# Start addresses of the tiles that TensorE reads, in one hybrid decoder layer on one core

## The chip, the core and the metric

The kernel runs on one core of one Trainium2 chip. The metric is the device time of one execution in microseconds (us). The kernel before took 2267.95 us, the median of three runs (2267.1 to 2267.99).

## What is computed

One decoder layer over 512 tokens of width 2048, in float32. Cut to what matters here:

```python
h = rmsnorm(x, attn_norm)                       # x: [512, 2048]
proj = h @ w_in                                 # 2048 x 5376: q, k, v of head groups A, B, C
# A: windowed softmax attention, B: stick-breaking attention, C: dilated softmax attention
mix = concat(rmsnorm(out_a), rmsnorm(out_b), rmsnorm(out_c))
x = x + mix @ w_out                             # 2048 x 2048
u = causal_dwconv(rmsnorm(x, ffn_norm) @ w_up)  # 2048 x 11264
gate, up = split(u)
x = x + (silu(gate) * up) @ w_down              # 5632 x 2048
```

The four weight products carry nearly all of the matrix work.

## The kernel before

**Products in three parts.** TensorE takes float32r operands (float32 whose low bits are cleared). Each weight and each activation is therefore split into a high part and the rest, and each product of two 128-row tiles is three matmuls: high by high, high by rest, rest by high (function mm3, lines 263 to 267). The stationary operand of a matmul is a 128x128 block of weights (512 bytes in each partition, out of a tile wh or wl of 2048 bytes), the moving operand is a 128x512 tile of activations (2048 bytes in each partition), and the result is one PSUM tile, 512 columns wide.

**The order of the work.** One stream of weight products runs from start to end: the projections of B, A and C, the output projection, and the feed-forward layer in six chunks of eight tiles, up-products and down-products taken in turns. The pieces of the weights (512 KB) are loaded by SyncE's queue (SP) into three buffers wr; ScalarE (ACT) copies half a piece into wh, VectorE (DVE) subtracts it from the raw weights into wl (function split, lines 251 to 261). Attention, norms and the gating run beside this stream. A planner at build time (classes Engine and Clock, lines 38 to 114) gives every instruction an estimated duration and issues each side task when its inputs should be ready, so the order on every engine is fixed when the program is built. The planner's cost of an instruction depends on its kind and its columns, not on an address.

**Which tiles move through TensorE.** The trace names tiles without numbers. In the projections of the heads (up to about 650 us) and in the output projection for the heads of A and B, the moving tiles are `x`: 32 tiles of 2048 bytes in pool xp. In the output projection for the heads of C they are `mc` (16 tiles in pool fp). In the feed-forward layer the up-products move `xg2`, which the trace prints as `xg` (32 tiles in pool fp); the down-products move `x` for the chunks 0, 2 and 4 and `mc` for 1, 3 and 5 (line 992). In attention the tiles st and akv (queries and keys), pt (weights of attention), vt and av (values), sq (squares), and the constant matrices trir, restr, bdr and cst are read.

**Where the tiles lie.** The framework lays the tiles of a pool one behind another in the order in which they are first made, each rounded up to 32 bytes, and pool behind pool in the order cp, wp, xp, then ap (attention), whose place fp takes over after attention. The first 1152 bytes of a partition are the framework's own. In cp stand sm (240 bytes, rounded to 256), cst (1536), trir, restr, bdr (512 each), r1 (2048), epsc, onec, gp (one slot of 32 bytes each) and two gacc (2048 each), so wp begins at 10720. Worked out in this way, the tiles start at these offsets:

| tiles | pool | first start | past a multiple of 512 | past a multiple of 2048 |
|---|---|---|---|---|
| wh, wl (stationary, blocks at steps of 512) | wp | 23008 | 480 | 480 |
| x (moving) | xp | 39392 | 480 | 480 |
| xg2 (moving) | fp | 106336 | 352 | 1888 |
| mc (moving) | fp | 178016 | 352 | 1888 |
| st, sq (moving; st also stationary) | ap | 106976 | 480 | 480 |
| pt, akv, vt, av (after the small tile tb of 96 bytes) | ap | 154176 | 64 | several |
| trir, restr, bdr, cst (stationary) | cp | 1408 | 384 | several |

xg2 and mc differ from x because fp begins with the tile conv, whose 1408 bytes are no multiple of 512.

Of the kernel before, what the change touches and what calls it, by code (L numbers as in the profile page):

```python
# [9 lines left out]
F32 = mybir.dt.float32  # L10
F32R = mybir.dt.float32r
# [9 lines left out]
EPS = 1e-6  # L21
NEG = -1e30

# columns of the packed small parameters
SM_AG, SM_FG, SM_MG, SM_G4, SM_SINK, SM_CONV, SM_N = 0, 16, 32, 48, 52, 60, 60 + 88 * 4
# columns of the packed constants
C_ID, C_ONE, C_MASK, C_TRI = 0, 128, 256, 384
NB = 640
# the least spacing of the heads of A, B, C, and what is added to each estimate
GAP = (8, 10, 10)  # L30
MARGIN = 0.08
# the order of the units of A and C
ORDER = "ACACACACCCCC"
# the order in which the output projection takes the tiles of heads: B, A, C
MIX_ORDER = list(range(4, 8)) + list(range(4)) + list(range(8, 16))


class Engine:
    """An engine whose instructions are timed by estimate as they are issued."""

# [38 lines left out]
class Clock:  # L79
    """Issues tasks beside the stream of matrix products, in the order of the estimated times:  # L80
    a task yields when what it has issued has to end before it goes on (or a time to wait)."""

# [34 lines left out]
def program(tc, xT, w_in, w_out, w_up, w_down, small, table, consts, onehot, lognum, out):  # L117
# [24 lines left out]
    with ExitStack() as ctx:  # L142
# [14 lines left out]
        trir = cp.tile([128, 128], F32R, name="trir")  # L157
        restr = cp.tile([128, 128], F32R, name="restr")
        bdr = cp.tile([128, 128], F32R, name="bdr")
        r1 = cp.tile([128, S], F32, name="r1")  # L160
        epsc = cp.tile([128, 1], F32, name="epsc")
        onec = cp.tile([128, 1], F32, name="onec")
        gp = cp.tile([128, 4], F32, name="gp")
        gacc = [cp.tile([128, S], F32, name="gacc", bufs=2) for _ in range(2)]
        gacc.append(gacc[1])

        # a slot is taken before its tile is made and given back after the tile's last use
        total = {"pj": 2, "s": 4, "po": 1, "c": 1, "qs": 3, "st": 9, "akv": 4, "vt": 2, "av": 1, "strip": 2,
                 "sc": 3, "pt": 6, "sq": 6, "o": 2, "mx": 3, "dn": 3, "nm": 3, "es": 2,
                 "cv": 3, "acc": 1, "rg": 1}  # L170
        # the shapes of the slots that are not rows
        shapes = {"sc": [128, 1280], "pt": [128, 1664], "vt": [128, 4, 2, 2, 64], "av": [128, 4, 2, 2, 64],
# [31 lines left out]

# [1 line left out]
        b_units = [(10 + p, 6 + p, 14 + p) for p in range(4)]  # L206
# [25 lines left out]
        raws, parts = {}, {}  # L232
# [9 lines left out]
        def split_next():  # L242
            """the next half of a piece of the weights"""
            i = at["split"]
            if i // 2 < len(stream):
                at["split"] = i + 1
                raw, arrival = raws[i // 2]
                n = raw.shape[1] // 2
                spawn(split(raw[:, i % 2 * n:i % 2 * n + n], arrival, i))
# [24 lines left out]
        def accumulate(pt, acts, ks, each=None):  # L274
            """the k tiles ks of a tile of a product, with the next weights of the stream"""
            half = min(len(acts), 8) // 2
            for k in ks:
                while acts[k] not in ready:
                    idle()
                if k % half == 0:  # L280
                    while at["use"] not in parts:
                        idle()
                    hi, lo = parts.pop(at["use"])
                    at["use"] += 1
                    split_next()
                mm3(pt, hi, lo, k % half, ready[acts[k]], k == 0, k == len(acts) - 1)
                if each:
                    each(k)
                clock.run()

        def product(acts, after):
            """one tile of a product; then the task after(tile)"""
            pt = begin()
            accumulate(pt, acts, range(len(acts)))
            spawn(after(pt))
            clock.run()

# [1 line left out]
        def rstd(pool, ss, n):  # L299
            """-2n * (ss / n + EPS) ** -0.5, with a Newton step after the tables"""  # L300
            y, a = yield from take(pool, "sq", 2)
            scalar.activation(y, ss, AF.Ln, bias=epsc, scale=1.0 / n)
            scalar.activation(y, y, AF.Exp, scale=-0.5)
            yield
            gpsimd.tensor_mul(a, y, y)
            yield
            vector.scalar_tensor_tensor(a, ss, n * EPS, a, op0=ALU.add, op1=ALU.mult)
            give(ss)
            vector.scalar_tensor_tensor(a, a, -3.0 * n, y, op0=ALU.add, op1=ALU.mult)
            give(y)  # L310
            return a
# [26 lines left out]

        nc.scalar.preload_act_table_set("natural_log_exp_and_others")
        vector.memset(epsc, EPS)  # L340
        vector.memset(onec, 1.0)

# [1 line left out]
        with ExitStack() as actx:  # L344
            ap = actx.enter_context(tc.tile_pool(name="ap", bufs=1))

            def strips():
                """the biases of the heads that softmax takes, in their order, as far ahead as there is room"""
                for head in strip_order:
                    g = yield from take(ap, "strip")  # L350
                    a = rb[head:head + 1, 0:1]
                    load(g, bass.AP(tensor=a.tensor, offset=a.offset, ap=[[1, 128], [1, S]]))
                    yield
                    ready["strip", head] = g
# [8 lines left out]
            def stacked(q, key):  # L363
                """for each head of the pair its high parts over its low parts"""
                res = yield from take(ap, "st", 2, F32R)
                for h in range(2):
                    scalar.copy(res[h][HALF[h]], q[HALF[h]])
                yield
                for h in range(2):
                    vector.tensor_sub(res[h][HALF[1 - h]], q[HALF[h]], res[h][HALF[h]].bitcast(F32))  # L370
                give(q)
                yield
                ready[key] = res

            def doubled(q, key):
                """for each head of the pair its high parts twice and its low parts twice"""
                tag = "akv" if key[0] == "ak" else "st"
# [87 lines left out]
            def softmax_head(q, dup, vt, h, o, head, sinks, window):  # L465
# [53 lines left out]
                def place(t, i, n):  # L519
                    if window:  # L520
                        # block (j, i) at 256 j + 128 (i - j), the last one after its zeros
                        base, step = ((0, 128), (128, 128), (384, 128), (640, 256))[i]
                    else:
                        # block (j, i) at 384 j + 128 i
                        base, step = 128 * i, 384
# [33 lines left out]

            # key blocks j of the stick-breaking heads: (j, first query, number of queries, column); in the operands of  # L560
            # products the last block follows columns of zeros
            BLK = [(0, 0, 512, 0), (1, 128, 384, 512), (2, 256, 256, 896), (3, 384, 128, 1152)]
# [82 lines left out]

            # heads in the order in which they run, at most three at a time
            heads = []
# [44 lines left out]
            def spill(g):  # L692
                """the normalised heads of a group in high and low parts, to wait for the slots of x"""
                tiles = (range(4), range(4, 8))[g]
# [30 lines left out]

            # x and the first three tiles of w_in, tile of x by tile of x
            acc = grab(ap, "o")
# [116 lines left out]
            def last_products(q_after, v_after):  # L844
                """the last two tiles, by halves of x, so that half of its slots are free early"""
                q, v = begin(), begin()
# [29 lines left out]

            # the output projection of the heads of B and A, beside the last heads of C
            xn = []
# [22 lines left out]
            while left[2]:  # L901
# [3 lines left out]
                else:  # L905
                    idle()
# [1 line left out]
        fp = ctx.enter_context(tc.tile_pool(name="fp", bufs=1, reuse_waits="tile"))  # L908
        cv = fp.tile([128, SM_N - SM_CONV], F32, name="conv")
        load(cv, small[:, SM_CONV:])  # L910

# [46 lines left out]

# [1 line left out]
        gs = {}  # L960
# [84 lines left out]
def _pieces(w):  # L1045
    """[K, N] as pieces of eight K tiles by one N tile, each [128, 8 * 128]"""
    k, n = w.shape
# [50 lines left out]
```

## Time and profile before

| | |
|---|---|
| median of three runs | 2267.95 us |
| profiled execution: its span, first to last instruction | 2265.6 us |
| what lies around the span, against the median | 2.35 us |
| TensorE busy, share of the span | 2254.7 us, 100% |
| matmuls | 10068 |
| VectorE busy; ScalarE busy | 1211.2 us, 53%; 981.9 us, 43% |
| granted TensorE clock, mean | 1.000 |

The span is that of one profiled execution; beside it only the run times are given. A matmul's own duration in the trace (about 395 ns for 512 columns) overlaps its neighbours', because matmuls are pipelined, so "TensorE busy" says only that one is always under way. What TensorE takes for a matmul is the step from the start of one to the start of the next, read from the starts in the timeline or from a piece of the chain divided by its count. The granted clock of 1.0 is 2.4 GHz; if one column is taken in each cycle, as the planner reckons (line 62: 4 ns and n/2400 us), 512 columns are 213.3 ns, and the step cannot be shorter than that.

### The profile page before, as it was taken

The page shows a single profiled execution, that of the slowest core. Times are in us where ns is not written, and L with a number is a line of the kernel's source. Part 1 is how long each engine was busy: PE and PEld are TensorE (multiplying, and loading weights), DVE is VectorE, ACT ScalarE, POOL GpSimd, SP SyncE. Part 2 cuts the span into 40 slices and gives each one's busy share as a digit, 9 for nine tenths or more (in the row PEclk, how much of TensorE's full clock was granted, in tenths as well). Part 3 has the DMA queues.
Part 4 walks back from the last instruction along what each step waited for, and adds up shares of the span by engine and source line. Part 5 has one row for each costly group of instructions (what it writes and reads, how often), then busy time and mean ns, then how long its engine had stood idle before and what let it go on. Part 6 is the DMA issues. An engine that isn't in the chain of part 4 may idle for free.

```text
span 2265.6 us, 27033 instructions
## 1 busy us (share of the span) xinstructions
PE 2254.7 (100%) x10068; PEld 1838.4 (81%) x10068; DVE 1211.2 (53%) x2090; ACT 981.9 (43%) x1864; POOL 100.8 (4%) x153
## 2 busy tenths in 40 slices
PE   8999999999999999999999999999999999999999
PEld 6888888888888878888888888888888888888887
DVE  7667777767755654544444444444444444443444
ACT  6778677776654433333323323332333233232322
POOL 4000101010100200000000000000000000000000
PEclk9999999999999999999999999999999999999999
DMA  6333343334743333323333322333332233333224
GB/s 196 95 94 98 121 146 112 110 103 162 227 159 98 93 94 94 98 96 93 93 95 100 94 93 93 93 93 94 101 94 93 93 93 96 97 95 94 93 86 137
DMA packets 83082, 244.26 MB, mean 108 GB/s; under 512 B 9784, under 2 KB 13240, under 8 KB 82952
## 3 DMA queue, kind: packets, MB, share of 16 engines
q1 hardware_dynamic: 82952, 242.55, 34.3%
q8 instruction: 79, 1.29, 0.2%
q14 instruction: 51, 0.42, 0.1%
HBM read 223.05 MB, written 12.64 MB: 104 GB/s over the span
## 4 chain that ended last, share of the span: by engine, by line
PE 98%; DMA 0%; DVE 0%; issue 0%; SPq 0%; ACT 0%; DVEq 0%; ACTq 0%
PE pj L49 92%; PE s L49 4%; PE po L49 2%; PE c L49 1%; SPq L127 0%; DMA st<-in_xT_dram 0%; DVE wl L49 0%; DMA wr<-in_w_in_dram 0%; DMA cst<-in_consts_dram 0%; ACT x L49 0%; DVE sq L49 0%; DVE x L49 0%; DVE o L49 0%; DVE pt L49 0%; DVE sc L49 0%
## 5 line engine op out<-in xcount | busy, mean ns | idle before, releaser
L49 ACT CAST wh<-wr 128x512 fp32r<-128x512 f32 (+2 forms) x782 | 475.3, 609 | 1114.8 <-PE pj L49 1031.9
L49 PE MATMUL pj<-xg,wh 128*128 128x512 f32 x2816 | 885.1, 395 | 0.0
L49 DVE TENSOR_TENSOR wl<-wr,wh 128x512 fp32r<-128x512 f32 (+2 forms) x782 | 539.4, 692 | 536.0 <-ACT wh L49 530.2
L49 PE MATMUL pj<-x,wh 128*128 128x512 f32 x2272 | 710.2, 394 | 0.0
L49 PEld LDWEIGHTS pj<-xg,wh 128*128 128x128 f32 x2816 | 528.6, 188 | 128.6 <-issue 0.5
L49 PE MATMUL pj<-xg,wl 128*128 128x512 f32 x1408 | 556.2, 395 | 0.0
L49 PEld LDWEIGHTS pj<-x,wh 128*128 128x128 f32 x2272 | 415.3, 188 | 81.4 <-issue 3.0
L49 PE MATMUL pj<-x,wl 128*128 128x512 f32 x1136 | 444.1, 391 | 0.0
L49 PEld LDWEIGHTS pj<-xg,wl 128*128 128x128 f32 x1408 | 264.3, 188 | 64.1
L49 PE MATMUL pj<-mc,wh 128*128 128x512 f32 x896 | 281.5, 395 | 0.0
L49 PEld LDWEIGHTS pj<-x,wl 128*128 128x128 f32 x1136 | 213.2, 188 | 46.1
L49 PEld LDWEIGHTS pj<-mc,wh 128*128 128x128 f32 x896 | 168.2, 188 | 40.9
L49 PE MATMUL pj<-mc,wl 128*128 128x512 f32 x448 | 177.0, 395 | 0.0
L49 DVE TENSOR_TENSOR x<-pj,x 128x512 f32<-128x512 f32 x112 | 77.4, 691 | 133.8 <-PE pj L49 133.8
L49 DVE SCALAR_TENSOR_TENSOR cv<-sq,conv,cv 128x511 f32<-128x511 f32 (+1 forms) x176 | 132.1, 751 | 28.2 <-ACT cv L49 25.1
L49 DVE TENSOR_TENSOR sq<-pj,r 128x512 f32<-128x512 f32 x88 | 60.9, 692 | 146.5 <-PE pj L49 146.4
L49 PEld LDWEIGHTS pj<-mc,wl 128*128 128x128 f32 x448 | 84.1, 188 | 20.5
L49 ACT ACTIVATE cv<-sq,conv 128x512 f32<-128x512 f32 x88 | 71.9, 817 | 29.0 <-DVE sq L49 29.0
L49 DVE CUSTOM_DVE_ANT_0 sc<-s,strip 128x128 f32<-128x128 f32 (+3 forms) x96 | 43.6, 455 | 75.5 <-PE s L49 75.2
L49 ACT ACTIVATE sc<-sc,nm 128x128 f32<-128x128 f32 (+2 forms) x96 | 50.2, 526 | 1.4 <-DVE nm L49 1.3
L49 ACT CAST pt<-s 128x128 fp32r<-128x128 f32 (+2 forms) x96 | 35.7, 398 | 26.8 <-PE s L49 26.3
L49 ACT ACTIVATE sc<-sc,dn 128x128 f32<-128x128 f32 (+2 forms) x96 | 43.5, 526 | 4.3 <-DVE dn L49 4.2
(115 smaller groups left out, 1316.6 us busy)
## 6 DMA issues: line engine op xcount, KB each, us to landing
wr<-in_w_up_dram SPq DMA_DIRECT2D x176, 512.0 KB, 3.5
wr<-in_w_down_dram SPq DMA_DIRECT2D x80, 512.0 KB, 3.4
wr<-in_w_in_dram SPq DMA_DIRECT2D x78, 512.0 KB, 3.6
wr<-in_w_out_dram SPq DMA_DIRECT2D x32, 512.0 KB, 3.5
st<-st SPq DMA_DIRECT2D x48, 128.0 KB, 4.4
strip<-rb SPq DMA_DIRECT2D x24, 256.0 KB, 4.0
st<-in_xT_dram SPq DMA_DIRECT2D x16, 256.0 KB, 3.9
o_dram<-o SPq DMA_DIRECT2D x16, 256.0 KB, 4.3
```

Source lines behind the costliest of these rows:

```text
L49: res = issue(out, *args, **kwargs)
```

## The change

Tiles of the pools are resized and moved; no instruction that computes is added or taken away.

- restr and bdr move from pool cp to the head of pool ap.
- epsc, onec and gp become parts of one tile `few` of 24 bytes.
- A tile `pad` of 152 columns (608 bytes) is added to cp, behind few, and filled with zeros once by VectorE; nothing reads it.
- conv in pool fp grows from 352 to 512 columns; the load fills the same 352.
- Comments are dropped (not shown).

```diff
+PAD = 152
@@ cp
         trir = cp.tile([128, 128], F32R, name="trir")
-        restr = cp.tile([128, 128], F32R, name="restr")
-        bdr = cp.tile([128, 128], F32R, name="bdr")
         r1 = cp.tile([128, S], F32, name="r1")
-        epsc = cp.tile([128, 1], F32, name="epsc")
-        onec = cp.tile([128, 1], F32, name="onec")
-        gp = cp.tile([128, 4], F32, name="gp")
+        few = cp.tile([128, 6], F32, name="few")
+        epsc, onec, gp = few[:, :1], few[:, 1:2], few[:, 2:]
+        pad = cp.tile([128, PAD], F32, name="pad")
         gacc = [cp.tile([128, S], F32, name="gacc", bufs=2) for _ in range(2)]
@@ before attention
         nc.scalar.preload_act_table_set("natural_log_exp_and_others")
+        vector.memset(pad, 0.0)
         vector.memset(epsc, EPS)
         vector.memset(onec, 1.0)
...
             ap = actx.enter_context(tc.tile_pool(name="ap", bufs=1))
+            restr = ap.tile([128, 128], F32R, name="restr")
+            bdr = ap.tile([128, 128], F32R, name="bdr")
@@ output projection
-        cv = fp.tile([128, SM_N - SM_CONV], F32, name="conv")
-        load(cv, small[:, SM_CONV:])
+        cv = fp.tile([128, 512], F32, name="conv")
+        load(cv[:, :SM_N - SM_CONV], small[:, SM_CONV:])
```

## Rows read from the trace of the kernel before

**Rows 1.** The page: span, TensorE's busy time, its clock in 40 slices.
```profile
span 2265.6 us, 27033 instructions
...
PE 2254.7 (100%) x10068; PEld 1838.4 (81%) x10068; DVE 1211.2 (53%) x2090; ACT 981.9 (43%) x1864; POOL 100.8 (4%) x153
...
PEclk9999999999999999999999999999999999999999
```
**Rows 2.** The waits of TensorE, all of them: us in total, times, longest.
```profile
PE s L49 <- ACT wh L49: 4.8, 1, 4.8
PE s L49 <- DVE wl L49: 1.5, 2, 0.9
PE po L49 <- DVE pt L49: 0.8, 1, 0.8
```
**Rows 3.** The chain that ended last, its longest piece: start, us, what.
```profile
798.69 1463.18 PE pj L49 x6303
```
**Rows 4.** Timeline of TensorE, moving tiles x: start, us, what, count merged.
```profile
664.82 0.61 PE L49 MATMUL pj<-x,wh 128*128 128x512 f32 x2
...
667.54 0.61 PE L49 MATMUL pj<-x,wh 128*128 128x512 f32 x2
```
**Rows 5.** Timeline of TensorE, moving tiles xg2 (as xg) and mc.
```profile
1180.26 0.63 PE L49 MATMUL pj<-xg,wh 128*128 128x512 f32 x2
...
1182.36 0.63 PE L49 MATMUL pj<-xg,wh 128*128 128x512 f32 x2
...
1300.03 0.63 PE L49 MATMUL pj<-mc,wh 128*128 128x512 f32 x2
...
1302.83 0.39 PE L49 MATMUL pj<-mc,wh 128*128 128x512 f32 x1
```
**Rows 6.** Groups of matmuls over the span: tiles, shape, count, busy, mean ns.
```profile
L49 PE MATMUL pj<-xg,wh 128*128 128x512 f32 x2816 | 885.1, 395 | 0.0
L49 PE MATMUL pj<-x,wh 128*128 128x512 f32 x2272 | 710.2, 394 | 0.0
L49 PE MATMUL pj<-xg,wl 128*128 128x512 f32 x1408 | 556.2, 395 | 0.0
L49 PE MATMUL pj<-x,wl 128*128 128x512 f32 x1136 | 444.1, 391 | 0.0
L49 PE MATMUL pj<-mc,wh 128*128 128x512 f32 x896 | 281.5, 395 | 0.0
L49 PE MATMUL pj<-mc,wl 128*128 128x512 f32 x448 | 177.0, 395 | 0.0
```
**Rows 7.** The same groups in the stretch 0 to 650 us, moving tiles x.
```profile
L49 PE MATMUL pj<-x,wh 128*128 128x512 f32 x1368 | 430.9, 396 | 0.0
```
**Rows 8.** The same groups in the stretch 798.7 to 2261.87 us, moving tiles x.
```profile
L49 PE MATMUL pj<-x,wh 128*128 128x512 f32 x768 | 236.7, 389 | 0.0
```
**Rows 9.** Timeline of TensorE: eight matmuls of one head's values, and the next.
```profile
308.22 1.47 PE L49 MATMUL po<-pt,vt 128*128 128x512 f32 x8
309.53 0.63 PE L49 MATMUL pj<-x,wh 128*128 128x512 f32 x2
```
**Rows 10.** Busy us (instructions) of PE, PEld, DVE, ACT, POOL in one stretch; PEclk; DMA.
```profile
60.00:650.00 590.00, 589.21 (x2904) 494.17 (x2903) 420.10 (x917) 428.81 (x972) 53.41 (x109) 1.00 0.41 125
```
**Rows 11.** Making and loading weights: idle time and its releaser; us to landing.
```profile
L49 ACT CAST wh<-wr 128x512 fp32r<-128x512 f32 (+2 forms) x782 | 475.3, 609 | 1114.8 <-PE pj L49 1031.9
...
wr<-in_w_up_dram SPq DMA_DIRECT2D x176, 512.0 KB, 3.5
```
**Rows 12.** Timeline of VectorE at the start: a memset, and the first wait.
```profile
0.80 0.06 DVE L49 MEMSET epsc<- 128x1 f32 x1 [0.80 <-PEq L1086]
...
4.39 0.75 DVE L49 SCALAR_TENSOR_TENSOR x<-st,sm,x 128x512 fp32r<-128x512 f32 x1 [3.50 <-ACT x L49]
```
**Rows 13.** Timeline of SyncE's queue: the load of conv and what follows.
```profile
668.76 0.42 SPq L127 DMA_DIRECT2D conv<-in_small_dram  x1
669.23 0.42 SPq L127 DMA_DIRECT2D x<-in_xT_dram  x1
```

## The prediction

> **What bounds the kernel now.** I read the page first: TensorE is under way for 2254.7 of 2265.6 us, and its clock is at the upper level, 2.4 GHz, in every slice [rows 1]. The waits come next: TensorE waits for another engine for 7.1 us in all, 6.3 of them for weights of the first products [rows 2]. So no engine holds TensorE up, and the time is the sum of the steps from one matmul to the next. The longest piece of the chain, 6303 matmuls in 1463.18 us, is 232.1 ns a matmul [rows 3]; 512 columns at one a cycle are 213.3 ns. Nearly 19 ns of each step are therefore neither a wait nor a column.
>
> The timeline shows what these 19 ns hang on. Where the moving tile is x, the starts at 664.82 and 667.54 us are twelve matmuls apart: 2.72 us / 12 = 226.7 ns [rows 4]. Where it is xg2, nine matmuls take 2.10 us, and where it is mc, twelve take 2.80 us: both 233.3 ns [rows 5]. In cycles these are 544 and 560, or 512 + 32 and 512 + 48. Shape, type, weight tiles (the same wh and wl buffers) and PSUM tiles are the same. That the two prices hold throughout is shown by the chain: after 798.69 us there are 768 + 384 = 1152 matmuls on x (two of wh to one of wl) [rows 8], the other 5151 of 6303 are on xg2 and mc, and 1152 x 226.67 + 5151 x 233.33 ns = 1463.0 us, against 1463.18 [rows 3]. By the table of addresses x starts 480 bytes past a multiple of 512 and the other two 352. So what differs is where the moving tile lies, and this is what the change moves.
>
> **The change, step by step.** First the addresses that it gives, by the same rule of laying out. cp becomes 256 + 1536 + 512 + 2048 + 32 + 608 + 4096 = 9088 bytes, and 1152 + 9088 = 10240 = 5 x 2048. wr, wh, wl and x are all multiples of 2048 long, so wh, wl and x start at multiples of 2048. With conv at 2048 bytes xg2 and mc do too. These serve the 4224 + 3408 + 1344 = 8976 matmuls on xg2, x and mc, of 10068 [rows 1, 6]. Not everything is moved as announced: restr and bdr put st and sq at multiples of 512 only; tb's 96 bytes put pt, vt, akv and av 96 past one; cst and trir stay at 384. I count nothing for all these: by the loops of the heads these are 32 x 8 matmuls of pt with vt or av, 8 x 14 with trir or restr and 8 x 8 of akv, 432 in all; at most 20 ns each, up or down, that is under 9 us.
>
> The step after the change is the one unknown that matters, since no row has a weight block and a moving tile that both start on a multiple of 512. In every row a weight block of 512 bytes lies across two units of 512, and a moving tile of four across five. Its bounds: from below 213.3 ns, one column a cycle; from above 233.3, the highest step of the long runs [rows 5], with the dearer case as a rival below. The nearest rows are those of x, 32 bytes from the next multiple: 32 cycles over [rows 4]; xg2 and mc, 160 bytes from it, are 48 over [rows 5]. The excess comes in whole 16s, and a tile on the boundary has no broken unit at either end, for weights nor for activations, which no row can say. I take the middle of 0 and 16 cycles: 520 cycles, 216.7 ns. The ends 213.3 and 220.0 stay for the range.
>
> The TensorE page of the Trainium skill (TensorE: Matmul & The Clock Gate, Back-to-back issue gap) states N/2.4 + 2.5 ns for matmuls of N columns in a row, 215.8 ns here, with no word on addresses; by an estimate from it the sum below would be 2139 us. The rows show 226.7 and 233.3, so that figure is not reached before the change.
>
> The sum at 216.7 ns:
> - xg2 and mc: (4224 + 1344) x 16.67 ns = 92.8 us [rows 5, 6].
> - x after 798.7 us: 1152 x 10.0 = 11.5 us [rows 8]. x in the output projection before that: all on x are 2272 + 1136 = 3408 [rows 6], 2052 of them before 650 us (1368 with wh [rows 7], half as many with wl), so 204 are left: 2.0 us.
> - x beside attention: 2052 x 10.0 = 20.5 us. Here other engines may hold TensorE up: ACT is busy for 428.8 of 590 us and DVE for 420.1 [rows 10], and TensorE's order is fixed. 4% less time would make 76% and 74%, so neither becomes the bound, but a chain of short steps that just ends in time now may end late. Late next would be the copies of PSUM tiles of a head, for which DVE's and ACT's shares leave room. I count three quarters, 15.4 us.
> - The three first products (tiles s, 144 matmuls) wait for loads: nothing.
>
> 92.8 + 11.5 + 2.0 + 15.4 = 121.7 us. The span of 2265.6 becomes 2143.9; with the 2.35 us around it, 2146 us. At 213.3 ns and all of the attention part it is 111.4 + 45.4 = 156.8 us, so 2111; at 220.0, with three quarters, 74.2 + 19.3 = 93.5, so 2174.
>
> What is costed at nothing. The memset of pad: epsc's, of one column, takes 0.06 us, and a DVE instruction of 512 columns 0.75 us; DVE then idles 3.50 us until ACT and the loads release it [rows 12]. Uncovered it would cost below 0.75 us. The planner adds 0.2 + 152/960 = 0.36 us to DVE's first estimate, so a few tasks of the first microseconds may be issued in another order; the waits there are 6.3 us in all [rows 2], and a change of that is within what lies around the sum. conv's load stands where it stood on SP's queue, with the same bytes; its tile now lies over restr, bdr and part of o0, before over o0 alone. The matrices are read last well before the load at 668.76 us, after the last head; the load of x behind it is issued at once [rows 13]. If it waited, the weights behind it would be late by that wait. The stream of weights: a piece of 512 KB serves 24 matmuls, 5.60 us at the present step and 5.20 after; a load lands in 3.5 us with three buffers, and ACT's copy waits for TensorE to give a buffer back for 1031.9 us [rows 11], so this stays ahead.
>
> **The rivals.**
> - *Only the distance between the two operands counts.* x lies 0 past wh modulo 512, xg2 and mc 128 short of it. After the change all lie at 0, so x's 226.7 becomes the step of all: 5568 x 6.67 = 37.1 us, 2231 us. For it: x is the nearest row, and the distance is the only thing that is the same before and after. Against it: pt and vt are at distance 0 too, both 64 past, and eight matmuls of 2 x (512 + 384 + 256 + 256) = 2816 columns, 1173 ns, take 1.31 us, 17 ns over each [rows 9], not 13.
> - *No effect*: the step hangs on something else that separates x from xg2 and mc, as their region of the memory, and stays: 2268 us. For it: xg2 and mc lie above x throughout. Against it: the regions meet at no round address, while the remainders differ plainly. The SBUF page of the Trainium skill (SBUF — State Buffer, Specifications) counts in cachelines of 16 bytes; 480 and 352 are both multiples of 16, so by it the change would gain nothing. The two steps of rows 4 and 5 speak against that.
> - *Slower*: two aligned operands hit each other. Suppose that a weight block and a moving tile are read at the same time, and that equal places in their units of 512 bytes collide, equal starts are then the worst case, and pt with vt, both on multiples of 64, are the sign: about 17 ns over [rows 9], above x's 13. Then x goes to 233.3 and xg2 and mc stay: 3408 x 6.67 = 22.7 us more, 2291 us. The place is every matmul on x; it decides if the excess at remainder 0 is above 42 cycles, for (3408 x 32 + 5568 x 48) / 8976 = 42 is today's mean. Against it: a conflict between two streams of fixed pace would not fit x's low step at distance 0.
>
> **How the numbers follow.** The forecast (both ends on the boundary, 0 to 16 cycles over, 2111 to 2174): 0.60. Distance alone, 2231: 0.23. No effect: 0.09. Slower: 0.08. Some 0.2% (4.5 us) is what runs of this kernel can tell. Faster is the first two, 0.83. The range takes both in, with some room at each end, 2105 to 2237, and leaves 0.17 out; the likeliest case alone is 2105 to 2178.
>
> **What would show it.** In the changed kernel, the starts of twelve matmuls in the feed-forward layer stand 2.60 us apart (2.80 and 2.72 before), equal for xg2, mc and x; the chain's piece after the norm is 6303 x 216.7 = 1366 us in place of 1463; the waits of TensorE grow by 5 us in attention. A step of 226.7 for all says distance; 233.3 for all says conflict; two different steps say that something else than these starts decides. The prediction is wrong if the step for xg2 is above 220.

## The result, and the profile after

The changed kernel took 2230.48 us, the median of four runs (2230.37 to 2230.58), against 2267.86 for the kernel before: a ratio of 0.9836 (95% interval 0.9822 to 0.985), 37.4 us less. The direction was forecast, the size was not: 122 us were, and 2230.48 lies near the far end of the range. One of the rivals, that only the distance between the two operands counts, had 2231 us.

The page of the changed kernel, its span and the busy times:

```profile
span 2228.6 us, 27035 instructions
...
PE 2217.2 (99%) x10068; PEld 1838.5 (82%) x10068; DVE 1211.9 (54%) x2091; ACT 983.8 (44%) x1864; POOL 100.7 (5%) x153
```

The same 10068 matmuls, one instruction more on VectorE (the memset of pad). The span is 37.0 us shorter, and TensorE's busy time 37.5 (it was 2254.7 before [rows 1]).

The waits of TensorE in the changed kernel, all of them (us in total, times, longest):

```profile
PE s L50 <- ACT wh L50: 5.0, 1, 5.0
PE s L50 <- DVE wl L50: 1.8, 2, 1.2
PE po L50 <- DVE pt L50: 0.8, 1, 0.8
```

7.6 us, where 7.1 were before [rows 2]: no wait came or went. So the 37 us are in the steps from one matmul to the next.

The longest piece of the chain that ended last (start, us, what):

```profile
796.16 1428.72 PE pj L50 x6303
```

The same 6303 matmuls as in [rows 3], now 1428.72 / 6303 = 226.67 ns each, 544 cycles, where the mean was 232.1. Before 796 us the kernel gained only 2.5 us (798.69 - 796.16).

The timeline of TensorE, first on x, then on xg2 (printed as xg):

```profile
663.67 0.61 PE L50 MATMUL pj<-x,wh 128*128 128x512 f32 x2
...
667.75 0.61 PE L50 MATMUL pj<-x,wh 128*128 128x512 f32 x2
...
1299.91 0.61 PE L50 MATMUL pj<-xg,wh 128*128 128x512 f32 x2
...
1302.63 0.61 PE L50 MATMUL pj<-xg,wh 128*128 128x512 f32 x2
```

On x eighteen matmuls take 4.08 us, 226.7 ns as before [rows 4]. On xg2 twelve take 2.72 us, 226.7 ns, where the step was 233.3 [rows 5]. The gain is that xg2 and mc became as fast as x: (4224 + 1344) x 6.67 ns = 37.1 us, of 37.4 measured. The boundary of 512 bytes itself, on which x and the weights now lie, changed nothing for x.

### The profile page after: what moved, and what is told of

Same layout as the page of the kernel before. It is cut to its first block, busy times and chain, and to the rows that moved or that the text cites. A ratio compares the mean times of both kernels' runs of the same rounds, so it can differ in the third digit from the quotient of the medians.

```text
span 2228.6 us, 27035 instructions
## 1 busy us (share of the span) xinstructions
PE 2217.2 (99%) x10068; PEld 1838.5 (82%) x10068; DVE 1211.9 (54%) x2091; ACT 983.8 (44%) x1864; POOL 100.7 (5%) x153
## 4 chain that ended last, share of the span: by engine, by line
PE 98%; DMA 1%; DVE 0%; issue 0%; SPq 0%; ACT 0%; DVEq 0%; ACTq 0%
PE pj L50 91%; PE s L50 5%; PE po L50 2%; PE c L50 1%; DMA wr<-in_w_in_dram 0%; DVE wl L50 0%; DMA st<-in_xT_dram 0%; SPq L128 0%; DVE sq L50 0%; DVE x L50 0%; ACT x L50 0%; DVE o L50 0%; DVE pt L50 0%; DVE sc L50 0%; ACT wh L50 0%
## 5 line engine op out<-in xcount | busy, mean ns | idle before, releaser
L50 PE MATMUL pj<-xg,wh 128*128 128x512 f32 x2816 | 867.3, 389 | 0.0
L50 PE MATMUL pj<-xg,wl 128*128 128x512 f32 x1408 | 547.7, 389 | 0.0
L50 PE MATMUL pj<-mc,wh 128*128 128x512 f32 x896 | 275.7, 389 | 0.0
```

What stands on the lines that cost most here:

```text
L50: res = issue(out, *args, **kwargs)
```

## The experiments

Two theories were put to the test. **Distance**: the step hangs on where the moving tile starts relative to the weight block, not on either start. **Alignment**: a start on a multiple of 512 is what helps, and x had been near enough to one. In what follows "at 64" means 64 bytes past a multiple of 512, and a step is given in cycles of 2.4 GHz. The distance is the start of the moving tile less that of the weight block, modulo 512. Steps in text and tables are worked out from the starts of matmuls in a row on one kind of tile, after 660 us.

### One line of the change alone

```diff
 (the kernel before)
-        cv = fp.tile([128, SM_N - SM_CONV], F32, name="conv")
-        load(cv, small[:, SM_CONV:])
+        cv = fp.tile([128, 512], F32, name="conv")
+        load(cv[:, :SM_N - SM_CONV], small[:, SM_CONV:])
```

> The kernel before with one edit: conv is 512 columns wide. Nothing starts on a multiple of 512; weights, x, xg2 and mc all lie 480 past one, at distance 0. 'Distance': all steps 544 cycles, the whole gain, 2230.5 us. 'Alignment': xg2 and mc stay off the boundary as x is, and a boundary is worth something only with the rest of the change: xg2 and mc as x, 544, but then the changed kernel with all on the boundary should have been below 544.

It took 2230.46 us, a ratio of 0.9835 (0.982 to 0.985): all of the gain, with weights, x, xg2 and mc all at 480. The chain's piece:

```profile
795.94 1428.70 PE pj L49 x6303
```

1428.70 us, as in the changed kernel. None of the four lies on a boundary of 512.

### All of the change but that line

```diff
 (the changed kernel)
-        cv = fp.tile([128, 512], F32, name="conv")
-        load(cv[:, :SM_N - SM_CONV], small[:, SM_CONV:])
+        cv = fp.tile([128, SM_N - SM_CONV], F32, name="conv")
+        load(cv, small[:, SM_CONV:])
```

> The changed kernel with conv back at 352 columns: weights and x on a multiple of 2048, xg2 and mc 384 past a multiple of 512. 'Distance': xg2 and mc at 560, the time of before, 2268 us. 'Alignment': x on the boundary and weights on it should save something against before on the 3408 matmuls of x: below 2268 by up to 45 us.

It took 2267.16 us, a ratio of 0.9997 (0.9988 to 1.0007): nothing. The chain's piece:

```profile
799.54 1462.40 PE pj L50 x6303
```

Weights and x lie on multiples of 2048, and the piece is within 0.8 us of what it was before (1463.18 [rows 3]), because xg2 and mc are at 384, at the distance of before. So aligning weights and x is worth nothing on its own, and the widening of conv is the whole of the change.

### Everything off the boundary, at distance 0

```diff
 (the changed kernel; all four kinds of tiles at 96)
-PAD = 152
+PAD = 48
...
-        cv = fp.tile([128, 512], F32, name="conv")
+        cv = fp.tile([128, 384], F32, name="conv")
```

> Weights, x, xg2 and mc all 96 past a multiple of 512 (an odd multiple of 32). 'Distance': 544 cycles for all, 2230.5 us. 'Alignment' in any form: above 544, at 560 for all 2290 us.

2230.13 us in one run. The chain's piece:

```profile
795.90 1428.71 PE pj L50 x6303
```

An odd multiple of 32 serves as well as a multiple of 2048, if both operands share it. This leaves no room for "alignment" in either form.

### The distance in steps of 32 bytes

Four kernels are the changed one with a small tile ahead of the first x, another width of conv and a small tile ahead of the first mc, so that the three moving tiles stand at three places and the weights stay on a multiple of 512. The first of them (in the other three padx has 64, 8 and 56 columns and padm 32, 16 and 16):

```diff
-PAD = 152
+PAD = 24
...
         vector.memset(pad, 0.0)
+        padx = xp.tile([128, 16], F32, name="padx")
+        vector.memset(padx, 0.0)
...
-        cv = fp.tile([128, 512], F32, name="conv")
+        cv = fp.tile([128, 400], F32, name="conv")
...
+            if not padm:
+                padm.append(fp.tile([128, 16], F32, name="padm"))
+                vector.memset(padm[0], 0.0)
             ready["mix", m] = scaled_split(t, sm[:, SM_MG + m:SM_MG + m + 1], *pair(fp, "mc", 16))
```

> Weights wh and wl stay on a multiple of 512; x is moved to 64, xg2 to 128 and mc to 192 bytes past one. Theory 'distance' (the step hangs on the distance from the weight block to the moving tile modulo 512, 544 cycles at 0 and 560 at 384): each tile gets its own step, 512 plus a multiple of 16; if the period is 256, xg2 at 128 stands with 384 and takes 560 cycles (233.3 ns). Theory 'alignment' (the start of a moving tile alone counts, 0 is the best): all three above 544, time above 2230 us, at 560 for all 2291 - 0 = about 2290 us.

> Weights on a multiple of 512; x at 256, xg2 at 320, mc at 448 past one. 'Distance' with a period of 256: x at 256 takes 544 cycles as at 0. With a period of 512: any multiple of 16 over 512. 'Alignment': all three above 544.

> Weights on a multiple of 512; x at 32, xg2 at 96, mc at 160 past one, odd multiples of 32. 'Distance': steps that fit between those of the even multiples of 32. 'Alignment' by 64 bytes: these three are dearer than 64, 128 and 192, by 16 cycles or more.

> Weights on a multiple of 512; x at 224, xg2 at 288, mc at 352 past one. 'Distance': steps that fit between those of the neighbours at 192, 256, 320 and 384. 'Alignment': above 544 for all three.

They took 2269.4, 2250.25, 2285.27 and 2284.14 us, beside 2267.85 for the kernel before. The timeline of the first, on x (at 64), xg2 (at 128) and mc (at 192):

```profile
664.53 0.63 PE L50 MATMUL pj<-x,wh 128*128 128x512 f32 x2
...
666.60 0.62 PE L50 MATMUL pj<-x,wh 128*128 128x512 f32 x2
...
1179.71 0.62 PE L50 MATMUL pj<-xg,wh 128*128 128x512 f32 x2
...
1182.49 0.64 PE L50 MATMUL pj<-xg,wh 128*128 128x512 f32 x2
...
1302.18 0.63 PE L50 MATMUL pj<-mc,wh 128*128 128x512 f32 x2
...
1304.98 0.40 PE L50 MATMUL pj<-mc,wh 128*128 128x512 f32 x1
```

Nine matmuls on x take 2.07 us (230.0 ns), twelve on xg2 2.78 (231.7), twelve on mc 2.80 (233.3). In the second run x lies at 256:

```profile
664.71 0.61 PE L50 MATMUL pj<-x,wh 128*128 128x512 f32 x2
...
667.43 0.61 PE L50 MATMUL pj<-x,wh 128*128 128x512 f32 x2
```

Here twelve take 2.72 us, 226.7 ns, as at distance 0. The medians over stretches of 24 matmuls in each whole run, in whole cycles, with those of the kernel before and of the changed one:

| distance, bytes | step, cycles | 256 more | step, cycles |
|---|---|---|---|
| 0 | 544 | 256 | 544 |
| 32 | 560 | 288 | 560 |
| 64 | 549 | 320 | 549 |
| 96 | 560 | 352 | 560 |
| 128 | 558 | 384 (before) | 560 |
| 160 | 562 | 416 | not run |
| 192 | 560 | 448 | 560 |
| 224 | 560 | 480 | not run |

The pattern repeats after 256 bytes, to within 2 cycles (128 and 384): 0 with 256 and 64 with 320 show it best. Distances that are a multiple of 256 are cheapest, 64 comes next, and all the rest pay 14 to 18 cycles. "Alignment by 64" falls too: 96 and 192 cost the same. And 64 is not 192: it matters which of the two starts is ahead.

These figures hide a pattern. In the kernel before every distance of mc is 384, and yet its steps take turns, whichever weight block comes next: one of 229 or 230 ns, one of 237 or 238 (1322 of 1326 steps). The means are 550 and 570 cycles, and 560 lies between them. In the changed kernel every step on mc is 226 or 227 ns. So at this distance a step hangs also on the step before it.

### Other starts, the same distances

Weights at 384, x at 64, xg2 at 384, mc at 0: three pads as above (PAD 120, padx 48, conv 464 and padm 32 columns).

> Weights 384 past a multiple of 512, x 64, xg2 384, mc 0. 'Distance' modulo 256 by the runs so far: x at 192 takes 560, xg2 at 0 takes 544, mc at 128 takes 558 to 560. 'Alignment' of the moving tile alone: mc 544 and xg2 560. A pair of starts that counts by itself (in the heads pt at 64 with restr at 384 had short steps): x below 544.

2256.34 us. The timeline on xg2 and on mc:

```profile
1900.18 0.62 PE L50 MATMUL pj<-xg,wh 128*128 128x512 f32 x2
...
1902.22 0.62 PE L50 MATMUL pj<-xg,wh 128*128 128x512 f32 x2
...
1299.74 0.63 PE L50 MATMUL pj<-mc,wh 128*128 128x512 f32 x2
...
1303.24 0.63 PE L50 MATMUL pj<-mc,wh 128*128 128x512 f32 x2
```

Nine matmuls on xg2 take 2.04 us (226.7 ns), fifteen on mc 3.50 (233.3). Over the run the steps were 560 for x (distance 192), 544 for xg2 (0) and 559 for mc (128). mc on a boundary is slow and xg2 off it is fast: distance, three times of three. The short steps of pt with restr (113 to 114 ns for 256 columns in the kernel before, 7 over 106.7) did not carry over to a long run.

### Is there a distance below 544?

The tiles of xg2 and mc get 8 more columns (32 bytes), and are read from 16 (xg2) and 8 (mc) bytes into them, so the tiles of each kind stand at eight distances (PAD is 24 and conv has 384 columns; shown is the function that makes the tiles):

```diff
+            if tag == "x":
+                return [pool.tile([128, S], F32R, name=tag, bufs=bufs) for _ in range(2)]
+            a = 4 if tag == "xg2" else 2
+            return [pool.tile([128, S + 8], F32R, name=tag, bufs=bufs)[:, a:a + S] for _ in range(2)]
```

> Weights and x on a multiple of 512. The tiles of xg2 and mc stand 2080 bytes apart and are read from 16 (xg2) and 8 (mc) bytes into them, so each has another distance from the weights: 16, 48, 80, ... and 8, 40, 72, ... modulo 256. Is there a distance with a step below 544? 'Distance, 0 is the least': the three steps of every tile are above 1632 cycles, some 1660 to 1685, and the time is near 2268. If an odd sixteenth is better than 0, some tiles show less than 1632.

2259.03 us, 9 us less than expected: the mean step on xg2 was 555 cycles, not 560. The three matmuls of a tile never took less than 1639 cycles on xg2 and 1654 on mc; so none reached 1632 (3 x 544), where x stayed. No distance below 544 was found.

### Which weight block counts

A tile of 128 bytes between wh and wl puts wl at 128; wh, x, xg2 and mc lie on multiples of 512 (PAD is 24, conv has 384 columns, and a tile of 384 bytes ahead of x makes up for the 128; shown is the edit of the weights).

```diff
                 hi = wp.tile([128, 384], F32R, name="wh", bufs=4)
+                if c == 0:
+                    padw = wp.tile([128, 32], F32, name="padw", bufs=1)
+                    vector.memset(padw, 0.0)
                 lo = wp.tile([128, 384], F32R, name="wl", bufs=4)
```

> wl lies 128 bytes past a multiple of 512; wh, x, xg2 and mc lie on one. 'Distance' as a meeting of the moving tile with one weight block: one of the three steps is longer by 14 to 16 cycles, the other two stay at 544, together 1646 to 1648, and the time is 2230 + 8976 / 3 x 15 / 2.4 ns = about 2249 us. The longer step shows which block counts: the step before the matmul of wl (its block is loaded while the matmul before it runs), or the matmul of wl itself. If the distance counts only for the first matmul of three, nothing changes.

2265.93 us, 17 us above what was expected. The chain's piece:

```profile
803.73 1456.72 PE pj L50 x6303
```

1456.72 / 6303 = 231.1 ns, 554.7 cycles in the mean. By their place in the three the steps on xg2 were 544.0, 558.0 and 562.0: the first matmul of wh is untouched, the second, beside which wl's block is read, has 14 cycles more, and wl's own, beside which the next wh is read, has 18 more. That read of wh takes 192 ns in the trace, the other two 188. So one block out of place is paid for twice. Neither of the two readings that were offered (the block being read, or the block in use) holds by itself. The first 14 cycles fit the block being read: 558 is the step at distance 128. The 18 fall where the block being read is at distance 0; that one step bears on the next, as in the kernel before, would do for them, but this run does not separate it from the block in use.

### A shorter read of weights

The rest of the weights is taken with 64 of its 128 columns (half of the rows of that product are left out), as the second of three matmuls; mc is at 128. The control has the same order with whole blocks. In both PAD is 24, conv has 384 columns and padm 32.

```diff
             tensor.matmul(pt, hi[:, c], act[0], start=first, stop=False)
-            tensor.matmul(pt, hi[:, c], act[1], start=False, stop=False)
-            tensor.matmul(pt, lo[:, c], act[0], start=False, stop=last)
+            tensor.matmul(pt[:64], lo[:, k * 128:k * 128 + 64], act[0], start=False, stop=False)
+            tensor.matmul(pt, hi[:, c], act[1], start=False, stop=last)
```

> Leaves out half of the rows of the product of the rest of the weights: its stationary block is 64 columns in place of 128 (and it stands second of the three matmuls). Weights, x and xg2 on a multiple of 512, mc 128 past one. If the excess is made while weights are read beside the moving tile, a shorter read makes less of it: the three steps on x and xg2 fall from 3 x 544 = 1632 cycles, by 16 if half of one excess of 32 goes; the three on mc fall from 1674 to 1680 by some 16 to 24; the time is some 20 us below 2230. If the excess belongs to the moving tile or to every matmul alike, 1632 and about 1677 stay, and the time is 2236 us (mc's 1344 matmuls at 558 to 560).

> The order of the run with half a block, but with whole blocks: high by high, rest by high, high by rest. Weights, x and xg2 on a multiple of 512, mc 128 past one. If the order alone made that run slow, the three steps on x and xg2 are about 1655 cycles here too, and the time is near 2258 us. If the half block made it slow, they are 1632 and mc's about 1677, the time 2236 us.

With half blocks 2258.54 us, with whole ones 2239.71. The second is the changed kernel's time and 1344 x 6.67 ns = 9.0 us for mc; the 2236 of the two expectations was summed too low. The mean of three steps on xg2 was 1655 cycles with half blocks and 1632 with whole ones: the shorter read made the time longer, against both theories of its expectation. On mc it made it a little shorter, 1674 cycles for 1680. The half block is read in 134 ns in place of 188, as the group of weight loads shows:

```profile
L50 PEld LDWEIGHTS pj<-xg,wh 128*128 128x128 f32 x2816 | 528.5, 188 | 193.7 <-issue 0.2
...
L50 PEld LDWEIGHTS pj<-xg,wl 128*64 128x64 f32 x1408 | 188.9, 134 | 60.1 <-issue 0.2
```

So the excess is not a price by the column of weights that is read. A half block also shifts when the read ends relative to the moving tile, which fits a matter of phase, but that was only argued.

## Why the prediction was wrong, point by point

- **What bounds the kernel**: right. TensorE's steps set the time before and after, and no wait took their place (7.6 us of waits).
- **The step hangs on the addresses**: right, and the two prices of 544 and 560 cycles were the whole matter: 5568 matmuls at 16 cycles less are the measured gain.
- **The addresses after the change**: right, also that st, pt and trir don't lie as announced. They carried no time that could be seen: with pt and vt at 96 in place of 64 the eight matmuls of [rows 9] take 1.30 us in the changed kernel, 1.31 before.
- **The step after the change** is what failed: "a tile on the boundary has no broken unit at either end [...] I take the middle of 0 and 16 cycles". The step was 544 cycles (226.7 ns), 32 over, above the 220 ns that were named as the sign of being wrong. The units of 512 bytes were a supposition that no row bore, and the whole 16s do not hold either (549, 558, 562; and 560 is a mean of 550 and 570): the table of addresses held two differences between x and the other two tiles, the start (480 against 352) and the distance from the weights (0 against 384), and one pair of steps cannot tell them apart. I took the start; the runs show that it is the distance, modulo 256. The nearest row, x, had the right price, and the two terms mis-sized by it are those of the sum: 92.8 us for xg2 and mc were 37, and 28.9 us for x were nothing.
- **The rival that came true** (2231, with 0.23) was put back by the eight matmuls of pt with vt, which have distance 0 and 17 ns over [rows 9]. They have 256 to 512 columns and stand between others; in the changed kernel they keep about 16 ns, (1300 - 1173) / 8, while the long runs at distance 0 have 13.3. The trace of the kernel before shows where the rest lies: over the 21 such groups behind a matmul on x the first two (512 columns) are 20 ns over, the last four (256 columns) 13. Steps on x behind the group are long at first too: 562 cycles for the first, 544 from the seventh on. In these rows the short step comes only some matmuls after a change of tiles; why is open. A short mixed group says little of a long run of one shape.
- **The slower rival** does not come about at distance 0; but it is what distances do that are no multiple of 256: with x off its distance the kernel takes up to 2285 us.
- **Beside attention** x's step counts for half. With all three tiles at 560 cycles (x at 224) 3408 x 6.67 = 22.7 us were due over the kernel before, and 2284.14 - 2267.85 = 16.3 came. After attention x has 1356 matmuls, 9.0 us, so the 2052 beside it paid 7.3 in place of 13.7. It is not hidden behind waits, for TensorE's waits are 7.1 us in the kernel before and 8.1 in that run. The cause lies in the steps: between 60 and 650 us the first three steps on x behind another kind of matmul take 582 cycles in the mean in the kernel before and 583 in that run, the next three 550 and 559, and only from the tenth on are they 544 and 560. Many pieces there are too short to come to the price of their distance. The quarter that the prediction left out, for engines that come late, was not put to the test, since x's step did not change.
- **Costed at nothing**: the memset, the moved matrices and conv's load cost nothing that shows (conv alone 2230.46, the whole change 2230.48).

## What to carry to other kernels

Where TensorE hardly ever waits and still takes more than a cycle a column, list the start addresses of both operands beside the steps, and change them one at a time. Here a moving tile should begin a multiple of 256 bytes from its weight block; a round address by itself was worth nothing, and one tile of an odd size (1408 bytes) at the head of a pool cost 1.6% of the time. When two tiles differ in two ways, a forecast from one pair of rows should price both readings alike.

## What the runs showed that was not expected

- TensorE's two operands are not independent. The Trainium skill (TensorE: Matmul & The Clock Gate, Step-by-step: what each phase is for) says that loading the next weights takes no read bandwidth from the running matmul. In these runs a step of 512 columns is 544 to 562 cycles by nothing but the distance of the two operands; the measurement decides. That the two reads collide is the likely reading, but no run shows a collision itself; the read of a whole weight block takes 188 ns in the kernel before and in the changed one, so the excess does not show there.
- The 16-byte cachelines of the Trainium skill (SBUF — State Buffer, Specifications) do not tell these starts apart: all distances of the table are multiples of 32, and the steps differ by 18 cycles.
- 32 cycles remain at the best distance, and neither a finer distance nor a shorter read removed them. Where they come from is open.
- One misplaced block of three lengthens two steps (14 and 18 cycles), and half a block costs more than a whole one (1655 against 1632 cycles for three).
- At distance 384 single steps are not alike: they alternate between 550 and 570 cycles on mc in the kernel before. And behind another kind of matmul the first three steps on x are long at distance 0 (582 cycles) and at 224 (583) alike.
